# Linear attention of a two-layer decoder: the gate's input by products of 32 columns, four side by side, and heads that begin when the head in front has issued its products

## The chip, the cores and the metric

The kernel runs on one core of a Trainium2 chip. The metric is the device time of one execution in microseconds (us); lower is better. The median of three runs before the change is 1902.51 us.

## The reference, cut to what matters

The program is a trunk of two decoder layers over 528 tokens (16 meta tokens and 512 others) of 1024 features, in float32. Layer 0 is: half a feed-forward network, chunked gated linear attention, half a feed-forward network. Layer 1 has sliding-window attention in the place of the linear attention. The change lies in the linear attention:

```python
def gla_mixer(hn, w_in, w_gate, b_gate, g_head, w_out):
    q, k, v, r, lr = jnp.split(hn @ w_in, [...], axis=-1)   # 512, 512, 1024, 1024, 16 columns
    gk = jax.nn.log_sigmoid((lr @ w_gate + b_gate).astype(jnp.float32)) / GLA_TAU
    ...
    bcum = jnp.cumsum(chunks(padf(gk), GLA_DK), axis=3)
    q_dec = qf * jnp.exp(bcum)
    k_dec = kf * jnp.exp(-bcum)
    att = jnp.where(causal, jnp.einsum('bhncd,bhnsd->bhncs', q_dec, k_dec), 0.0)
    o_intra = jnp.einsum('bhncs,bhnsv->bhncv', att, vf)
    ...                                                       # state passed from chunk to chunk
    o = o_intra + jnp.einsum('bhncd,bhndv->bhncv', q_dec, states)
    o = rmsnorm(o, g_head) * jax.nn.silu(r.astype(jnp.float32)).reshape(B, L, GLA_HEADS, GLA_DV)
    return o.reshape(B, L, GLA_V).astype(hn.dtype) @ w_out
```

`hn` is the normalised residual stream. There are 4 heads with 128 key and 256 value features each. `lr` has 16 columns; its product with `w_gate` gives the forget gate of every key feature.

## The kernel before

Activations are kept transposed: 128 features on the partitions, tokens along the row. The residual stream is `H` (8 tiles of 128 features by 528 tokens), and `Y` is a second array of that size, which holds values, head outputs and projections. Tokens are treated in two groups, `L0 = [(0, 272), (272, 256)]`.

**Products in split precision.** Weights come from memory in units of 128 output columns by 1024 input features (512 KB, two transfers of 256 KB). ScalarE copies each half into a rounded part and VectorE subtracts for the remainder (lines 234 and 235). The operand `x_l0m` is built from `H` in the same way (`Operand.build`, lines 448 and 449): the residual times the norm's gain, without the row factor. `mm3s` makes three products for each 128x128 block (high by high, low by high, high by low), so a unit over both groups is 8 x 3 x 2 = 48 products, `x<-x_l0m,w` in the profile, at line 170 as all products are. The row factor `x.rt` (`R_l0m`) is applied when a result is read out of PSUM; it is ready per group only after sums of squares, a small root on POOL and a broadcast product (`st_l0m`, `r_l0m`).

**Order.** TensorE's order is fixed when the program is built. `Flow` is a planner with a clock: every product advances it by an estimated cost, and generators (jobs) that `yield` a delay or another job are resumed when the clock has come to it (`flow.pump()`, called between products). The constants at the head of the file (`BEHIND`, `ADDED`, `CHAIN` and so on) are such delays. The other engines' orders come from the tile framework, by dependences and program order. SBUF scratch is a pool of 32 equal buffers (`pair_tile`; `duo` gives the two halves of one), PSUM has 8 banks (`ps`). Weight units are loaded ahead in the order of the list `units`, as far as `set_ahead` allows.

**The linear attention, `gla`.** `GLA_ORDER` gives the order of the 25 units of the input weight: unit 24 holds the 16 columns for `lr`, filled up with zeros to 128; 4 to 7 are k, 0 to 3 q, 8 to 15 v, 16 to 23 r.
- `x_first` makes the products of four units together, first for group 0 and then for group 1, as `x_l0m` is built: `lr`, k and q of head 0, and the first v tile. Their results are evacuated when the row factor of the group is done (the jobs `drained`).
- `gates` waits for those, multiplies `lr` with `w_gate` (products `z`, 128 rows of which 16 hold something), and forms the log-sigmoid with Abs, Tanh and Ln on ScalarE and a few operations on VectorE.
- The second v tile is one unit of `x_units`, which makes its products at once and hands the evacuation to a job where the row factor is late.
- `core(h)` is one head: two running sums of the gate (`TENSOR_TENSOR_SCAN`), transposed values (`pv`, `pm`), decayed keys and queries (`d`, `f`, `c`; Exp on ScalarE, products on VectorE), transposed keys (`pk`), scores (`pa`, `pb`), chunk states (`ps`), outputs (`po`, `pn`), and then the head's norm: squares on ScalarE, sums (`st_go`), root, broadcast (`r_go`) and scaling of `Y`. In the last head the two squared tiles of a group are summed by TensorE and the root is on VectorE; in the others POOL adds them and has the root.
- The loop spawns `core(h)`, which waits for the gates, for late evacuations and for the whole of `core(h-1)`, and then makes the four units of the next head, between whose products the planner puts those of `core(h)`.
- Eight units of r follow (`gated`): silu, times the head's normalised output, split into `og`. A tile waits for its own head if that is head 0 or 1, and for the last head otherwise. Then comes the output projection (`y<-og`).

Of the kernel before, what the change touches and what calls it, by code (L numbers as in the profile page):

```python
# [13 lines left out]
ALU = mybir.AluOpType  # L14
AX = mybir.AxisListType

P = 128
D = 1024
KD = 8
# [7 lines left out]
HEADS = 4  # L27
RSQRT_MAGIC = float(0x5F3759DF)
L0 = [(0, 272), (272, 256)]
# [16 lines left out]
ADDED = 1.4  # L46
LONGER = 0.8
BEHIND = 2.2
NORM = 4.0
SHUT = 5.0  # L50
LAG = 5
PERIOD = 3.2
SLOWER = 4.0
# [5 lines left out]
V_GAIN = 0  # L59
# [2 lines left out]
V_GN = 108  # L62
V_SINK = 110
V_N = 126
GLA_ORDER = [24, 4, 0, 8, 9, 5, 1, 10, 11, 6, 2, 12, 13, 7, 3, 14, 15] + list(range(16, 24))


class Flow:
# [63 lines left out]
def trunk_kernel(ctx: ExitStack, tc, a, out):  # L132
    nc = tc.nc
    pe, act, dve, pool, sp = nc.tensor, nc.scalar, nc.vector, nc.gpsimd, nc.sync
    flow = Flow()
# [7 lines left out]
    H = cp.tile([P, KD, TOK], F32, name="H")  # L143
    Y = cp.tile([P, KD, TOK], F32, name="Y")
    vec = cp.tile([P, V_N], F32, name="vec")
# [12 lines left out]
    def duo(name):  # L158
        t = pair_tile(name, F32)
        return t[:, 0], t[:, 1]  # L160
# [237 lines left out]
    def rstd(sq, n, dim, half, name, eng=pool, more=0.0):  # L398
        yy = root(sq, n, dim, name, eng)
        c, nch = yy.shape  # L400
        dg = sm.tile([P, 272], F32, tag="dg", name=f"dg_{name}", bufs=2)
        eng.tensor_tensor(
            dg[:c, :n].rearrange("p (j c) -> p j c", c=c),
            (hident if half else ident)[:c, :c].unsqueeze(1).to_broadcast([c, nch, c]),
            yy.unsqueeze(2).to_broadcast([c, nch, c]),
            op=ALU.mult,
        )
        yield (DCHAIN if eng is dve else CHAIN) + more
        r = ps(f"r_{name}")
        mm(r[:, :n], ones[:c, :], dg[:c, :n])  # L410
        return r
# [3 lines left out]
    def square_into(sums, src, i, count, name, parts=2):  # L415
        n = src.shape[-1]
        if i == 0 or i == count - 1 and parts == 2:
            sums.append(sm.tile([P, 272], F32, tag="acc", name=f"acc_{name}", bufs=6))
            act.activation(sums[-1][:, :n], src, AF.Square)
            return  # L420
        t = sm.tile([P, 272], F32, tag="sq", name=f"sq_{name}", bufs=2)
        act.activation(t[:, :n], src, AF.Square)  # L422
        pool.tensor_tensor(sums[0][:, :n], sums[0][:, :n], t[:, :n], op=ALU.add)  # L423
# [431 lines left out]
    def gla(x, finish):  # L855
        set_ahead(10)
        with tc.tile_pool(name="gp", bufs=1) as gp:
            wg, att = duo("wg")
            wg = wg[:, :512]
# [8 lines left out]
            def resets():  # L868
# [2 lines left out]
                    pool.memset(mt[:, META::st], 0.0)  # L871
                pool.memset(att, 0.0)
                yield 0
            lr = duo("lr")[0]
            qk, ls = {}, {}

            def evac(kind, h, g, p):
                o, n = g
                r = x.rt[:, o : o + n]
                if kind == "lr":  # L880
                    dve.tensor_tensor(lr[:, o : o + n], p[:, :n], r, op=ALU.mult)
                elif kind in "qk":
                    if h not in qk:
                        qk[h] = duo(f"qk{h}")
                    d = qk[h][kind == "k"][:, o : o + n]
                    if kind == "q":
                        dve.scalar_tensor_tensor(d, p[:, :n], 128 ** -0.5, r, op0=ALU.mult, op1=ALU.mult)
                    else:
                        dve.tensor_tensor(d, p[:, :n], r, op=ALU.mult)
                else:  # L890
                    dve.tensor_tensor(Y[:, h, o : o + n], p[:, :n], r, op=ALU.mult)

            def gates(drained):
                for j in drained:
# [22 lines left out]
            blk = lambda t: t[:, META:].rearrange("p (b c) -> p b c", c=P)  # L917

            def core(h, before):
                last = h == HEADS - 1  # L920
                for j in before:
                    yield j
                tau = 1.0 / 16.0
# [96 lines left out]
                for gi, (o, n) in enumerate(L0):  # L1020
                    accs.append([])
                    for i in range(2):
                        square_into(accs[gi], Y[:, 2 * h + i, o : o + n], i, 2, f"go{h}_{gi}", 1 + last)
                yield 2.0 + (0 if last else ADDED)
                def scale(gi, o, n):
                    eng, more = (dve, gi * BEHIND) if last else (pool, BEHIND)
                    r = yield from rstd(accs[gi], n, 256, True, f"go{h}_{gi}", eng, more)
                    dve.tensor_tensor(
                        yy[:, :, o : o + n], yy[:, :, o : o + n],
                        r[:, :n].unsqueeze(1).to_broadcast([P, 2, n]), op=ALU.mult,  # L1030
                    )
# [3 lines left out]

            og, rg = [None] * KD, [None] * KD
            cores = []

            def gated(m, g, p):
                o, n = g  # L1040
# [10 lines left out]
                dve.scalar_tensor_tensor(gs, gs, gn, Y[:, m, o : o + n], op0=ALU.mult, op1=ALU.mult)  # L1051
                split(og[m], gs, g)

            kinds = [("lr", 0), ("k", 0), ("q", 0), ("v", 0)]
            drained = x_first(x, 4, lambda i, g, p: evac(*kinds[i], g, p), first_ahead=5)
            flow.spawn(resets())
            gate = flow.spawn(gates(drained))
            late = x_units(x, 1, L0, lambda i, g, p: evac("v", 1, g, p))
            for h in range(HEADS):
                cores.append(flow.spawn(core(h, [gate] + late + cores[h - 1 : h])))  # L1060
                if h + 1 < HEADS:
                    kk = [("k", h + 1), ("q", h + 1), ("v", 2 * h + 2), ("v", 2 * h + 3)]
                    late = x_units(x, 4, L0, lambda i, g, p, kk=kk: evac(*kk[i], g, p))
# [357 lines left out]
def _tiles(w, kt, mt):  # L1421
    return w.reshape(kt, P, mt, P).transpose(2, 1, 0, 3).reshape(mt, P, kt * P)


def _layout(x, meta_tokens, norm_gains, w_ffn_in, w_ffn_out, gla_w_in, gla_w_gate, gla_b_gate, gla_norm,
            gla_w_out, kv_norm, w_kv, swa_w_q, swa_sinks, swa_w_out):
    c = {}
    c["h"] = np.concatenate([meta_tokens, x[0]], axis=0).T.reshape(KD, P, TOK).transpose(1, 0, 2)
    c["w_in"] = (
        w_ffn_in.reshape(2, 2, KD, P, 2, NFF, P).transpose(0, 1, 5, 4, 3, 2, 6).reshape(2, 2, NFF, 2, P, D)  # L1430
    )
    wo = w_ffn_out.reshape(2, 2, NFF, P, KD, P).transpose(0, 1, 4, 3, 2, 5)
    c["w_out"] = wo[:, :, :, :, :LAST].reshape(2, 2, KD, P, LAST * P)
    c["w_last"] = (
        wo[:, :, :, :, LAST:].transpose(0, 1, 2, 4, 3, 5).reshape(2, 2, NLAST, KD, P, P)
        .transpose(0, 1, 2, 4, 3, 5).reshape(2, 2, NLAST, P, D)
    )
    gin = np.zeros((D, 25 * P), np.float32)
    gin[:, : gla_w_in.shape[2]] = gla_w_in[0]
    c["gla_in"] = _tiles(gin, KD, 25)  # L1440
    wg = np.zeros((P, 512), np.float32)
    wg[:16] = gla_w_gate[0]
    c["w_gate"] = wg
    c["gla_out"] = _tiles(gla_w_out[0], KD, KD)
    c["w_kv"] = _tiles(w_kv, KD, 4)
    c["w_q"] = (
        swa_w_q[0].reshape(KD, P, 2, 2, 4, 64).transpose(2, 4, 1, 0, 3, 5).reshape(KD, P, D)
    )
    c["swa_out"] = (
        swa_w_out[0].reshape(2, 2, 4, 64, 4, 2, P).transpose(0, 4, 1, 3, 5, 2, 6).reshape(KD, P, D)  # L1450
    )
    vec = np.zeros((P, V_N), np.float32)
    vec[:, V_GAIN : V_GAIN + 96] = norm_gains.reshape(96, P).T
    vec[:, V_KVN : V_KVN + 8] = kv_norm.reshape(8, P).T
    vec[:, V_BG : V_BG + 4] = gla_b_gate[0].reshape(4, P).T
    vec[:, V_GN : V_GN + 2] = gla_norm[0].reshape(2, P).T
    vec[:, V_SINK : V_SINK + 16] = np.broadcast_to(
        swa_sinks[0].reshape(2, 2, 4).transpose(0, 2, 1).reshape(1, 16), (P, 16)
    )
    c["vec"] = vec  # L1460
    i, j = np.arange(P)[:, None], np.arange(P)[None, :]
    c["ident"] = np.eye(P, dtype=np.float32)
    c["gmask"] = ((i <= j) & (i // 64 == j // 64)).astype(np.int32)
    c["mgt"] = (j > i).astype(np.int32)
    c["mle"] = (i <= j).astype(np.float32)
    c["rowmask"] = (i // META == np.arange(8)[None, :]).astype(np.float32)
    ang = np.arange(TOK, dtype=np.float32)[:, None] * np.array(INV_FREQ, np.float32)[None, :]
    cos, sin = np.cos(ang).T.astype(np.float32), np.sin(ang).T.astype(np.float32)
    ct, st = np.ones((P, TOK), np.float32), np.zeros((P, TOK), np.float32)
    for r in (0, 64):  # L1470
        ct[r : r + 8], ct[r + 8 : r + 16] = cos, cos
        st[r : r + 8], st[r + 8 : r + 16] = -sin, sin
    c["cos"], c["sin"] = ct, st
    c["sel"] = np.zeros((P, 32), np.float32)
    for e in range(2):
        c["sel"][64 * e : 64 * e + 16, 16 * e : 16 * e + 16] = np.eye(16)
    c["cosp"], c["sinp"] = np.tile(np.concatenate([cos, cos]), (8, 1)), np.tile(np.concatenate([-sin, sin]), (8, 1))
    return {n: np.ascontiguousarray(v) for n, v in c.items()}
# [20 lines left out]
```

## Time and profile before

| | us |
|---|---|
| median of 3 runs (1901.91 to 1903.7) | 1902.51 |
| profiled execution | 1902.08 |
| its span | 1900.2 |
| first and last input product of the linear attention | 376.5 and 577.3 |

The profile is one execution, recorded by the hardware. In a row of the timeline the columns are: start and length in us from the span's start, engine, line, operation, result and operands, shapes and count; what stands in brackets at the end is the idle time in front and who ended it. Neighbouring rows of TensorE overlap, since products are pipelined; a slot is measured from start to start. A full fp32 product is recorded as two instructions, one in split precision (fp32r) as one.

### The profile page before, as it was taken

The page shows a single profiled execution, that of the slowest core. Times are in us where ns is not written, and L with a number is a line of the kernel's source. Part 1 is how long each engine was busy: PE and PEld are TensorE (multiplying, and loading weights), DVE is VectorE, ACT ScalarE, POOL GpSimd, SP SyncE. Part 2 cuts the span into 40 slices and gives each one's busy share as a digit, 9 for nine tenths or more (in the row PEclk, how much of TensorE's full clock was granted, in tenths as well). Part 3 has the DMA queues.
Part 4 walks back from the last instruction along what each step waited for, and adds up shares of the span by engine and source line. Part 5 has one row for each costly group of instructions (what it writes and reads, how often), then busy time and mean ns, then how long its engine had stood idle before and what let it go on. Part 6 is the DMA issues. An engine that isn't in the chain of part 4 may idle for free.

```text
span 1900.2 us, 37641 instructions
## 1 busy us (share of the span) xinstructions
PE 1876.1 (99%) x14642; PEld 1795.0 (94%) x14642; DVE 1403.1 (74%) x2825; ACT 1016.7 (54%) x2268; POOL 189.7 (10%) x374
## 2 busy tenths in 40 slices
PE   8999999999999999999999999999999999999997
PEld 8999999999999999999999898989987898989897
DVE  6885858766574798585887886868766779868584
ACT  5653536653245565363574553535756855636363
POOL 2000000321111300000033000000320140000002
PEclk9999999999999999999999999999999999999999
DMA  4333333422113123333351223233421212333331
GB/s 164 96 98 102 92 105 99 130 79 73 51 57 111 46 79 95 100 95 105 97 178 45 67 85 116 90 111 100 134 73 51 68 46 73 107 103 106 101 112 45
DMA packets 102931, 175.13 MB, mean 92 GB/s; under 512 B 11872, under 2 KB 24928, under 8 KB 102752
## 3 DMA queue, kind: packets, MB, share of 16 engines
q1 hardware_dynamic: 101920, 172.07, 28.9%
q8 instruction: 115, 1.88, 0.4%
q10 hardware_dynamic: 832, 0.65, 0.1%
q14 instruction: 64, 0.52, 0.1%
HBM read 170.05 MB, written 2.10 MB: 91 GB/s over the span
## 4 chain that ended last, share of the span: by engine, by line
PE 87%; DVE 8%; ACT 2%; issue 2%; POOL 0%; DMA 0%; SPq 0%; DVEq 0%; ACTq 0%; POOLq 0%
PE y L170 29%; PE a L170 19%; PE x L170 18%; PE c L170 8%; PE d L170 5%; DVE raw L259 1%; PE o L170 1%; ACT w_s L253 1%; DVE w_s L254 1%; DVE w L254 1%; PE e L170 1%; DVE w L235 1%; PE po L170 1%; PE sa L170 1%; PE ps L170 0%
## 5 line engine op out<-in xcount | busy, mean ns | idle before, releaser
L254 DVE TENSOR_TENSOR w_s<-raw,w_s 128x512 fp32r<-128x512 f32 x288 | 193.7, 690 | 130.5 <-ACT w_s L253 127.9
L170 PE MATMUL y<-hidl0f,w 128*128 128x256 f32 (+1 forms) x2112 | 262.3, 285 | 1.1 <-DVE hidl0f L428 0.9
L170 PEld LDWEIGHTS y<-hidl0f,w 128*128 128x128 f32 x2112 | 259.2, 188 | 2.2 <-DVE hidl0f L428 1.5
L253 ACT ACTIVATE w_s<-raw 128x512 fp32r<-128x512 f32 x288 | 175.1, 628 | 150.8 <-DVE raw L259 137.7
L235 DVE TENSOR_TENSOR w<-raw,w 128x512 fp32r<-128x512 f32 x378 | 236.3, 655 | 21.8 <-ACT w L234 20.0
L170 PE MATMUL y<-hidl1f,w 128*128 128x512 f32 (+1 forms) x1344 | 250.8, 346 | 0.3
L170 PEld LDWEIGHTS y<-hidl1f,w 128*128 128x128 f32 x1344 | 212.3, 188 | 34.9 <-DVE hidl1f L848 1.5
L234 ACT ACTIVATE w<-raw 128x512 fp32r<-128x512 f32 x378 | 207.5, 586 | 41.3 <-PE y L170 29.3
L423 POOL TENSOR_TENSOR acc_post<-acc_post,sq_post 128x256 f32<-128x256 f32 (+1 forms) x77 | 63.6, 826 | 1471.9 <-ACT sq_post L422 1471.2
L259 DVE TENSOR_TENSOR raw<-raw,raw 128x512 f32<-128x512 f32 x288 | 197.9, 687 | 5.5
L254 DVE TENSOR_TENSOR w<-raw,w 128x512 fp32r<-128x512 f32 x216 | 148.2, 687 | 29.9 <-ACT w L253 29.1
L170 PE MATMUL x<-x_l0m,w 128*128 128x272 f32 (+1 forms) x1200 | 158.2, 288 | 0.0
L253 ACT ACTIVATE w<-raw 128x512 fp32r<-128x512 f32 x216 | 134.0, 621 | 41.4 <-PE y L170 41.1
L170 PEld LDWEIGHTS x<-x_l0m,w 128*128 128x128 f32 x1200 | 149.3, 189 | 1.0
L625 DVE TENSOR_TENSOR Y<-y,Y 128x256 f32<-128x256 f32 (+2 forms) x176 | 82.3, 473 | 72.3 <-PE y L170 71.7
L170 PE MATMUL a<-zl0f_t,w_s 128*128 128x264 f32 x864 | 117.3, 285 | 0.0
L170 PE MATMUL a<-zl1f_t,w_s 128*128 128x256 f32 x864 | 114.7, 282 | 0.9 <-ACT c L823 0.8
L170 PEld LDWEIGHTS a<-zl0f_t,w_s 128*128 128x128 f32 x864 | 110.2, 188 | 0.2 <-ACT c L823 0.2
L170 PEld LDWEIGHTS a<-zl1f_t,w_s 128*128 128x128 f32 x864 | 107.4, 188 | 2.7 <-ACT c L823 2.3
L170 PE MATMUL x<-x_l0f,w 128*128 128x256 f32 (+1 forms) x768 | 100.7, 292 | 6.8 <-ACT w L234 6.0
L170 PEld LDWEIGHTS x<-x_l0f,w 128*128 128x128 f32 x768 | 97.6, 193 | 8.0 <-ACT w L234 6.0
L170 PE MATMUL x<-x_l1f,w 128*128 128x256 f32 (+1 forms) x576 | 93.0, 321 | 0.0
(497 smaller groups left out, 3243.9 us busy)
## 6 DMA issues: line engine op xcount, KB each, us to landing
raw<-in_w_in SPq DMA_DIRECT2D x352, 256.0 KB, 2.9
raw<-in_w_out SPq DMA_DIRECT2D x96, 256.0 KB, 3.4
raw<-in_gla_in SPq DMA_DIRECT2D x50, 256.0 KB, 3.2
raw<-in_w_last SPq DMA_DIRECT2D x48, 256.0 KB, 3.1
raw<-in_w_out SPq DMA_DIRECT2D x64, 128.0 KB, 2.9
raw<-in_gla_out SPq DMA_DIRECT2D x16, 256.0 KB, 2.7
raw<-in_w_q SPq DMA_DIRECT2D x16, 256.0 KB, 3.7
raw<-in_swa_out SPq DMA_DIRECT2D x16, 256.0 KB, 3.4
```

Of the source, the lines that this page charges most:

```text
L170: inst = pe.matmul(o, lhs, rhs, start=start, stop=stop, skip_group_check=onto)
L234: act.activation(w[:, 0, :m], raw[:, :m], AF.Copy)
L235: dve.tensor_tensor(w[:, 1, :m], raw[:, :m], w[:, 0, :m].bitcast(F32), op=ALU.subtract)
L253: act.activation(w[:, 0, :512], src, AF.Copy)
L254: dve.tensor_tensor(w[:, 1, :512], src, w[:, 0, :512].bitcast(F32), op=ALU.subtract)
L259: dve.tensor_tensor(dst, dst, src, op=ALU.add)
L423: pool.tensor_tensor(sums[0][:, :n], sums[0][:, :n], t[:, :n], op=ALU.add)
L625: dve.tensor_tensor(y, p[:, :n], y, op=ALU.add)
```

## The change

It has two parts.

The gate's input no longer has a unit of its own. The 16 columns of `lr` are padded to 32 and come unsplit in one block, `w_low` (128 x 8 x 32, 128 KB), which VectorE multiplies by the norm's gain. `low_rank` then multiplies it with `H` in full fp32, 8 products of 32 columns per token group: contraction tile k writes the PSUM partitions of strip k % 4, so that four products lie side by side, and each strip sums two tiles. `w_gate` stands four times on the partitions, so that the gate product `z` sums the four strips. The results are read out when both row factors are done, and `gates` waits for that too. The place of the old unit in `x_first` is taken by the second v tile, and no unit is made behind it before the units of head 1.

A head now waits for `mids[h-1]`, a job that the head in front finishes right behind its last output products and squares, in place of the whole of that head. The last head is treated as the others: POOL adds its squares and has the root.

```diff
-GLA_ORDER = [24, 4, 0, 8, 9, 5, 1, 10, 11, 6, 2, 12, 13, 7, 3, 14, 15] + list(range(16, 24))
+GLA_ORDER = [4, 0, 8, 9, 5, 1, 10, 11, 6, 2, 12, 13, 7, 3, 14, 15] + list(range(16, 24))
...
-            lr = duo("lr")[0]
+            lr, low = duo("lr")
+            low = low[:, : KD * 32].rearrange("p (k c) -> p k c", c=32)
+            sp.dma_start(low, a["w_low"])
...
-                if kind == "lr":
-                    dve.tensor_tensor(lr[:, o : o + n], p[:, :n], r, op=ALU.mult)
-                elif kind in "qk":
+                if kind in "qk":
...
+            def low_rank():
+                gains = vec[:, V_GAIN + 16 : V_GAIN + 16 + KD]
+                dve.tensor_tensor(low, low, gains.unsqueeze(2).to_broadcast([P, KD, 32]), op=ALU.mult)
+                yield LOW
+                banks = [ps(f"lr_{o}") for o, _ in L0]
+                for (o, n), p in zip(L0, banks):
+                    for k in range(KD):
+                        c = slice(k % 4 * 32, k % 4 * 32 + 32)
+                        mm(p[c, :n], low[:, k], H[:, k, o : o + n], k < 4, k >= 4, cost=0.14)
+                for job in x.rjob:
+                    yield job
+                for (o, n), p in zip(L0, banks):
+                    dve.tensor_tensor(lr[:, o : o + n], p[:, :n], x.rt[:, o : o + n], op=ALU.mult)
...
             def core(h, before):
-                last = h == HEADS - 1
...
-                        square_into(accs[gi], Y[:, 2 * h + i, o : o + n], i, 2, f"go{h}_{gi}", 1 + last)
-                yield 2.0 + (0 if last else ADDED)
+                        square_into(accs[gi], Y[:, 2 * h + i, o : o + n], i, 2, f"go{h}_{gi}", 1)
+                mids[h].finish(flow)
+                yield 2.0 + ADDED
                 def scale(gi, o, n):
-                    eng, more = (dve, gi * BEHIND) if last else (pool, BEHIND)
-                    r = yield from rstd(accs[gi], n, 256, True, f"go{h}_{gi}", eng, more)
+                    r = yield from rstd(accs[gi], n, 256, True, f"go{h}_{gi}", pool, BEHIND)
...
+            mids = [Job(None) for _ in range(HEADS)]
...
-            kinds = [("lr", 0), ("k", 0), ("q", 0), ("v", 0)]
+            kinds = [("k", 0), ("q", 0), ("v", 0), ("v", 1)]
             drained = x_first(x, 4, lambda i, g, p: evac(*kinds[i], g, p), first_ahead=5)
             flow.spawn(resets())
-            gate = flow.spawn(gates(drained))
-            late = x_units(x, 1, L0, lambda i, g, p: evac("v", 1, g, p))
+            gate = flow.spawn(gates(drained + [flow.spawn(low_rank())]))
+            late = []
             for h in range(HEADS):
-                cores.append(flow.spawn(core(h, [gate] + late + cores[h - 1 : h])))
+                cores.append(flow.spawn(core(h, [gate] + late + mids[h - 1 : h])))
...
+    low = np.zeros((D, 32), np.float32)
+    low[:, :16] = gla_w_in[0][:, 24 * P :]
+    c["w_low"] = low.reshape(KD, P, 32).transpose(1, 0, 2)
+    wg = np.zeros((4, 32, 512), np.float32)
+    wg[:, :16] = gla_w_gate[0]
+    c["w_gate"] = wg.reshape(P, 512)
```

The new constant `LOW = 1.0` is the planner's delay between the scaling of the block and its products.

More of the change, by code (lines that the diff above doesn't have):

```diff
@@ L50 @@
 SHUT = 5.0
+LOW = 1.0
 LAG = 5
@@ L1437, in _layout @@
     )
[L1438 to L1443, printed above, removed]
+    c["gla_in"] = _tiles(gla_w_in[0][:, : 24 * P], KD, 24)
+    low = np.zeros((D, 32), np.float32)
[4 more added lines that the diff above has]
+    c["w_gate"] = wg.reshape(P, 512)
     c["gla_out"] = _tiles(gla_w_out[0], KD, KD)
```

## The prediction

> **What bounds the kernel now.** I read the page's totals and chain first, then the linear attention stage in the table by stretches, then the waits of TensorE in that stage, and last its timeline, because the change touches no other stage.
>
> ```profile
> span 1900.2 us, 37641 instructions
> ...
> PE 1876.1 (99%) x14642; PEld 1795.0 (94%) x14642; DVE 1403.1 (74%) x2825; ACT 1016.7 (54%) x2268; POOL 189.7 (10%) x374
> ...
> PE 87%; DVE 8%; ACT 2%; issue 2%; POOL 0%; DMA 0%; SPq 0%; DVEq 0%; ACTq 0%; POOLq 0%
> ```
>
> TensorE is busy for 99% of the span and carries 87% of the chain that ended last. The table by stretches (columns: stretch, length, then busy time of PE, PEld, DVE, ACT, POOL) covers the stage:
>
> ```profile
> 376.50:400.00 23.50, 23.50 (x195) 23.37 (x194) 18.86 (x51) 14.87 (x37) 12.93 (x28) 1.00 0.12 35
> 400.00:427.00 27.00, 27.00 (x211) 26.43 (x210) 15.07 (x31) 13.08 (x22) 3.28 (x13) 1.00 0.34 108
> 427.00:466.00 39.00, 39.00 (x316) 37.71 (x315) 23.08 (x44) 13.43 (x28) 8.18 (x27) 1.00 0.22 69
> 466.00:506.00 40.00, 40.00 (x324) 38.51 (x323) 20.64 (x41) 12.60 (x27) 6.60 (x27) 1.00 0.21 66
> 506.00:546.00 40.00, 40.00 (x324) 38.58 (x323) 26.94 (x61) 15.93 (x38) 8.36 (x27) 1.00 0.13 41
> 546.00:578.00 32.00, 32.00 (x263) 30.68 (x262) 23.29 (x69) 13.88 (x31) 0.00 (x0) 1.00 0.22 67
> ```
>
> From 376.5 to 578 us TensorE has no idle time and the granted clock is 1.00; VectorE is at 52 to 80%, ScalarE at 32 to 63%. The waits of TensorE in and around the stage are one, at its end:
>
> ```profile
> PE y L170 <- DVE og L428: 0.4, 1, 0.4
> ```
>
> So a product that goes from this stage shortens the kernel by its own slot, as long as no new wait opens. Earlier heads by themselves are worth nothing here: the waits of one head are already filled with input products.
>
> **The products that go.** Unit 24 of the input weight holds 16 useful columns in 128. It takes 8 (contraction) x 3 (split precision) x 2 (token groups of 272 and 256) = 48 products. A run of input products that alternates between both groups gives their slot:
>
> ```profile
> 427.54 8.99 PE L170 MATMUL x<-x_l0m,w 128*128 128x272 f32 x72
> 436.37 0.60 PE L182 MATMUL pk<-ident,f 128*128 128x128 f32 x4
> ```
>
> 72 products take 436.37 - 427.54 = 8.83 us from start to start, 0.1226 each; 48 of them are **5.9 us**. The unit's place among the first four is taken by the second v unit, which was a unit of its own behind them, so nothing else is added or lost there.
>
> **The products that come.** 16 products in full fp32, 128 x 32 weights, 272 or 256 columns, in rounds of four that write partitions 0-31, 32-63, 64-95 and 96-127. The sliding-window part of this kernel has the same form, four products of 32 columns side by side (each recorded as two):
>
> ```profile
> 1392.69 0.64 PE L170 MATMUL turn<-q,sel 128*32 128x256 f32 x8
> 1393.26 2.97 PE L170 MATMUL x<-x_l1m,w 128*128 128x256 f32 x23
> ...
> 1441.57 1.06 PE L170 MATMUL turn<-q,sel 128*32 128x512 f32 x8
> 1442.56 0.30 PE L182 MATMUL ptm<-ident,mt 128*64 128x128 f32 x1
> ...
> L170 PEld LDWEIGHTS turn<-q,sel x24: 106/108/109, 1392.7 to 1441.6; 128*32 128x32 f32 x24
> ```
>
> Four at 256 columns hold TensorE for 0.57 us, four at 512 for 0.99. That is 0.42 us per 256 columns and 0.15 us fixed. Two rounds at 272 (0.60) and two at 256 (0.57) make **2.3 us**. The lower bound pays the fixed part once: 2 x 0.45 + 2 x 0.42 + 0.15 = 1.9. The upper bound puts the 0.108 us weight load of the last row in front of every one of the 8 passes on top of 2.3, 3.2. I take 2.3, since the rows have the same shape and precision.
>
> The Trainium skill ("TensorE: Matmul & The Clock Gate", Part 3, The mechanism) says that a weight load overlaps running products only when its row group differs, and here all four strips use all rows; by that rule all eight loads would show, and the block would be an estimated 1.74 us of columns and 8 x 0.108, 2.6 us. The trace speaks against it mildly: the two loads of a round, with the change of shape, cost 0.15 us together, less than 2 x 0.108.
>
> **The rest of the low-rank path.** The 32 columns come by one 128 KB transfer issued at the head of the stage, right behind the gate weight. Nothing is queued behind it on SyncE that is urgent, as its timeline shows:
>
> ```profile
> 361.68 0.33 SPq L860 DMA_DIRECT2D wg<-in_w_gate  x1
> 395.14 10.14 SPq L302 DMA_DIRECT2D raw<-in_gla_in  x12
> ...
> wg<-in_w_gate SPq DMA_DIRECT2D x1, 256.0 KB, 2.6
> ```
>
> The next weight is issued long after it, and the gate weight landed in 2.6 us, so the block is there well before it is used at about 402 us. It occupies half of a buffer that was taken anyhow for the low-rank result, though some 30 us earlier. VectorE scales it once (256 elements per partition, about 0.4 us), and loses two of the 128x512 splits of the old unit; ScalarE loses two copies. Cost on the path: zero, bounded by 0.5 us above if VectorE reaches the scaling late behind weight splits, and zero below, as TensorE waits for neither today.
>
> The evacuation of the low-rank result moves behind both row factors. The first group used to be done early; now both follow the second factor:
>
> ```profile
> 415.31 1.94 PE L170 MATMUL z<-lr,wg 128*128 128x272 f32 x8
> ...
> 411.89 0.42 DVE L881 TENSOR_TENSOR lr<-x,R_l0m 128x256 f32<-128x256 f32 x1 [2.95 <-ACT R_l0m L471]
> ```
>
> The gate products z start 3.0 us after that evacuation ended (412.31), because the planner waits for all drains of the first four units, which stay. One or two operations of 0.42 us more in front fit into the 3.0 us. Cost zero; the gates, and so head 0, begin when they do now.
>
> **The heads.** Head h+1 is released where head h has issued its last products, not where its normalisation is done. For heads 0 and 1 that is, in the timeline:
>
> ```profile
> 424.34 0.60 PE L182 MATMUL pv<-ident,Y 128*128 128x128 f32 x4
> ...
> 451.48 5.00 PE L170 MATMUL x<-x_l0m,w 128*128 128x256 f32 x39
> ...
> 466.24 0.60 PE L182 MATMUL pv<-ident,Y 128*128 128x128 f32 x4
> ...
> 475.75 0.60 PE L182 MATMUL pk<-ident,f 128*128 128x128 f32 x4
> ```
>
> A head takes 27 us from its first transposes (424.3) to its last products (451.5), and 14.8 us more until the next begins (466.2). Head 1 can begin at 451.5; its own input units are then issued, since they stand one unit further forward. Head 2 follows at 479 and head 3 at 506, or up to 6 us later where its input units come later than that. Its products then end by 539 and its normalisation by 554, some 20 us before the input products, which end near 578 now, the end of the last stretch of the table, and about 4 us earlier then. TensorE does the same products in another order, so the sum is zero, with two exceptions at the end.
>
> First, the last head now forms its sum of squares as the others do, by adding on POOL, which halves the products of that step:
>
> ```profile
> 456.32 1.04 PE L170 MATMUL st_go<-ones,acc_go 128*68 128x1 f32 x12
> ...
> 572.96 1.98 PE L170 MATMUL st_go<-ones,acc_go 128*68 128x1 f32 x24
> ```
>
> 1.98 us becomes 1.04: **0.94 us** less. The root on POOL in place of VectorE is longer, but the 20 us behind it cover that.
>
> Second, the one wait of the stage goes:
>
> ```profile
> 580.75 35.29 PE L170 MATMUL y<-og,w 128*128 128x272 f32 x283 [0.38 <-DVE og L428]
> ...
> 578.30:590.00 11.70, 11.28 (x89) 10.81 (x88) 11.23 (x25) 9.04 (x23) 0.00 (x0) 1.00 0.31 90
> ```
>
> VectorE is at 96% there, because the gated tiles 4 to 7 all wait for the last head. They are then spread over the input units before: **0.38 us** less, at best. Late next is the last gated tile alone, hidden behind the first output products.
>
> **Sum:** -5.9 + 2.3 - 0.94 - 0.38 = -4.9 us. The profiled execution took 1902.08 us for its span of 1900.2; the median of the runs is 0.43 above it. 1902.51 - 4.9 = **1897.6 us**.
>
> **The rivals.** *The four strips run one after another.* Then a round costs four times its 0.57, and the block 9.3 us: +9.3 - 5.9 - 0.94 - 0.38 = +2.1, 1904.6 us, no measurable change. The turn rows speak against it (four products in the time of one and a bit); what they don't have is an accumulation of two rounds into one strip. Chance 0.05.
>
> *The handover opens small waits.* A head's vector work has only a limited cover. For head 0, which began its scans with nothing in front of it, the rows on VectorE are:
>
> ```profile
> 427.88 1.25 DVE L926 TENSOR_TENSOR_SCAN b<-resets,ls 128x528 f32<-128x528 f32 x1
> ...
> 434.19 0.57 DVE L954 TENSOR_TENSOR f<-f,qk 128x400 f32<-128x400 f32 x1
> ...
> 453.18 1.25 DVE L926 TENSOR_TENSOR_SCAN b<-resets,ls 128x528 f32<-128x528 f32 x1
> ```
>
> That is 6.9 us from scan to the keys f that the transposes pk need. For head 1 pk stands 9.5 us behind pv, and its scans ran 13 us ahead of pv. With the new order the scans may lose that lead, and then 2.6 us of cover are left, shared with the normalisation of the head in front on ScalarE and the weight splits on VectorE. One us lost at each of three handovers gives 1900.6 us, by the bound below no change. VectorE's 52 to 59% in the stretches from 427 to 506 speaks against it. Chance 0.22.
>
> *The handover becomes the bound (slower).* The same mechanism, beyond its cover: ScalarE first does the tail of the head in front, VectorE first the weight splits, and the keys come late. From a delay of 2.6 us on TensorE stops, and from 2.6 + 2.9 = 5.5 us per handover the three cost 8.7 us, net +3.8. With 6 us of delay the three cost 10.2: 1907.8 us; at 7 us it would be 1910.8. For it: the operations share buffers that the head in front frees only with its last products. Against it: over 40% of VectorE and two thirds of ScalarE are idle in those stretches. Chance 0.13.
>
> **How the numbers follow.** A measurement of this kernel can tell 0.2%, 3.8 us, from no change: faster is below 1898.7, slower above 1906.3. The forecast has the remaining 0.60; its own range is 1896.0 to 1898.7. The lower end takes 0.4 us for the block at 1.9, 0.6 us if the 283 output products (35.29 / 283 = 0.1247 each) come down to the 0.1226 of the input products once VectorE is less crowded beside them, and 0.6 us of scatter, the distance of the fastest run, 1901.91, from the median. The 8-in-10 range goes up into the small waits, to 1901.8, and leaves out the slower rival, the serial strips and a little on either side. Faster 0.62 (the forecast and the mildest small waits), same 0.25, slower 0.13.
>
> **What would show it.** In the changed profile: 1152 input products in place of 1200; 32 records of the new products in about 2.3 us, starting within 30 ns of one another by fours; z within 1 us of where it stands; pv of head 1 near 451 us; the last head's r_go 15 us or more before the first y<-og; no wait there; and y<-og starting 4 to 5 us earlier. The prediction is wrong if TensorE shows waits ahead of pk, pa or pv, or if the new products wait for their scaled block.

## The result, and the profile after

The changed kernel takes **1896.94 us** (median of 7 runs, 1895.95 to 1897.11) against 1903.14 us for the kernel before (7 runs), 6.2 us less; the ratio is 0.9965, 95% interval 0.9956 to 0.9975. The prediction was 1897.6 us in a range of 1896.0 to 1901.8, with 0.62 on faster by over 0.2%. Ratios, here and below, are of fast runs; one run of e5_heads_later, 3353.32 us at a mean clock of 0.786, was in a slower state and stands in no ratio.

The page's totals and chain, after:

```profile
span 1895.3 us, 37597 instructions
...
PE 1871.5 (99%) x14614; PEld 1789.4 (94%) x14614; DVE 1400.4 (74%) x2802; ACT 1015.6 (54%) x2268; POOL 199.1 (11%) x400
...
PE 87%; DVE 8%; ACT 2%; issue 1%; POOL 0%; DMA 0%; DVEq 0%; ACTq 0%; POOLq 0%
```

TensorE is still the bound, with 28 records less (48 input products and 12 sum records go, 32 come). The stage in the table by stretches:

```profile
400.00:427.00 27.00, 27.00 (x227) 25.40 (x226) 14.53 (x30) 13.85 (x24) 2.76 (x12) 1.00 0.26 87
427.00:466.00 39.00, 39.00 (x320) 37.41 (x319) 26.67 (x56) 16.33 (x35) 9.00 (x27) 1.00 0.20 68
466.00:506.00 40.00, 40.00 (x314) 37.72 (x312) 24.49 (x47) 14.24 (x32) 10.87 (x30) 1.00 0.21 67
```

The list of TensorE's waits from 360 to 690 us, whole:

```profile
PE y L171 <- DVE hidl0f L429: 0.3, 1, 0.3
```

TensorE has no idle time; the wait at the first output products is gone, and the one that is left belongs to the feed-forward part behind. VectorE and POOL are busier from 427 to 506 us, where heads now overlap. The timeline of TensorE:

```profile
376.00 4.29 PE L171 MATMUL x<-x_l0m,w 128*128 128x272 f32 x33
...
403.62 1.99 PE L171 MATMUL lr<-H,lr 128*32 128x272 f32 x32
405.54 4.30 PE L171 MATMUL x<-x_l0m,w 128*128 128x272 f32 x33
...
450.76 0.60 PE L183 MATMUL pv<-ident,Y 128*128 128x128 f32 x4
...
551.95 1.06 PE L171 MATMUL r_go<-dg_go,ones 68*128 68x272 f32 x4
552.65 20.41 PE L171 MATMUL x<-x_l0m,w 128*128 128x256 f32 x165
572.90 36.71 PE L171 MATMUL y<-og,w 128*128 128x272 f32 x297
609.44 0.60 PE L171 MATMUL st_post_l0f<-ones,acc_post 128*68 128x1 f32 x8
```

The stage, from the first input product to the first output product, lasts 572.90 - 376.00 = 196.90 us, where it was 201.64 (376.63 to 578.27): -4.74. The first part of the output projection, up to st_post_l0f, lasts 36.54, where it was 37.60 (578.27 to 615.87): -1.06. So the change is worth 5.8 us in the trace. The span falls by 4.9. Two differences outside this stretch make up the rest: the opening was 0.63 us shorter, which adds to the gain, and later the granted clock was halved for one stretch, which the execution before did not have and which takes more away. TensorE's timeline where it starts:

```profile
1513.39 0.44 PE L171 MATMUL o<-pt,dv 128*64 128x128 f32 x4 [0.88 <-DVE pt L1288]
```

The stretch behind it in the table (the last columns are the granted clock, 0.50, and the DMA's share and rate):

```profile
1514.90:1518.20 3.30, 3.30 (x16) 2.79 (x14) 1.54 (x5) 0.50 (x2) 0.00 (x0) 0.50 0.00 0
```

It lies in the sliding-window part, behind a wait that both kernels have, and set the rest of the program back by 1.55 us, as the shift between the two traces shows (counted from the first product, 6.16 us ahead in front of it, 4.61 behind it).

### The profile page after: what moved, and what is told of

Same layout as the page of the kernel before. It is cut to its first block, busy times and chain, and to the rows that moved or that the text cites. A ratio compares the mean times of both kernels' runs of the same rounds, so it can differ in the third digit from the quotient of the medians.

```text
span 1895.3 us, 37597 instructions
## 1 busy us (share of the span) xinstructions
PE 1871.5 (99%) x14614; PEld 1789.4 (94%) x14614; DVE 1400.4 (74%) x2802; ACT 1015.6 (54%) x2268; POOL 199.1 (11%) x400
## 4 chain that ended last, share of the span: by engine, by line
PE 87%; DVE 8%; ACT 2%; issue 1%; POOL 0%; DMA 0%; DVEq 0%; ACTq 0%; POOLq 0%
PE y L171 29%; PE a L171 19%; PE x L171 18%; PE c L171 8%; PE d L171 5%; DVE raw L260 1%; PE o L171 1%; ACT w_s L254 1%; DVE w_s L255 1%; DVE w L255 1%; PE e L171 1%; DVE w L236 1%; PE po L171 1%; PE sa L171 1%; PE ps L171 0%
## 5 line engine op out<-in xcount | busy, mean ns | idle before, releaser
L171 PE MATMUL x<-x_l0m,w 128*128 128x272 f32 (+1 forms) x1152 | 152.3, 289 | 0.0
L171 PEld LDWEIGHTS x<-x_l0m,w 128*128 128x128 f32 x1152 | 143.5, 189 | 1.5 <-issue 0.4
```

Of the source, the lines that this page charges most:

```text
L171: inst = pe.matmul(o, lhs, rhs, start=start, stop=stop, skip_group_check=onto)
```

## The experiments

The stage's length and the listed waits at r_go, the broadcast of a head's norm, are the two numbers to compare, each from one profile; the ratios are against the kernel before on the same chip, whose median was 1903.02 us for e1 to e4, 1902.92 for e5 to e9 and 1903.90 for e10 and e11.

| kernel | median us | ratio, 95% interval | stage us | wait at r_go us |
|---|---|---|---|---|
| before | 1903.14 | | 201.64 | none |
| changed | 1896.94 | 0.9965 (0.9956 to 0.9975) | 196.90 | none |
| e1_low_alone | 1909.25 | 1.0033 (1.0020 to 1.0045) | 207.71 | 6.8 |
| e2_heads_alone | 1904.80 | 1.0012 (1.0004 to 1.0021) | 206.12 | 3.4 |
| e3_last_on_pe | 1903.32 | 1.0001 (0.9992 to 1.0010) | 202.60 | 2.9 |
| e4_one_strip | 1906.09 | 1.0018 (1.0009 to 1.0027) | 205.97 | 2.2 |
| e5_heads_later | 1902.09 | 0.9992 (0.9983 to 1.0002) | 200.59 | none |
| e6_earlier | 1899.90 | 0.9984 (0.9976 to 0.9993) | 200.95 | 2.3 |
| e8_margin | 1899.77 | 0.9984 (0.9975 to 0.9993) | 199.97 | 1.4 |
| e9_last_dve_later | 1897.69 | 0.9970 (0.9959 to 0.9981) | 197.84 | none |
| e10_later | 1898.44 | 0.9968 (0.9956 to 0.9981) | 196.83 | none |
| e11_roots_dve | 1896.18 | 0.9963 (0.9949 to 0.9976) | 196.85 | none |

**e1_low_alone: the low-rank part alone.** Against the changed kernel (the lines of the last head's sums and root are those of before as well):

```diff
-                cores.append(flow.spawn(core(h, [gate] + late + mids[h - 1 : h])))
+                cores.append(flow.spawn(core(h, [gate] + late + cores[h - 1 : h])))
```

> The changed kernel with its second part undone: a head waits for the whole of the head in front, and the last head has its squares summed by TensorE and its root on VectorE, as before. Theory (two separate sums of TensorE slots): 48 input products of 5.9 us go, the block of 1.92 us comes, so 4.0 us faster than the kernel before; the last head ends with the input products as before, and the first 18 output products again lose about 1.1 us to late gated tiles. Rival (the low-rank part gains only because the heads were moved with it): under 2 us faster, with a new wait of TensorE in front of the gates or of the first head.

It is 6.2 us slower than the kernel before. The theory falls: the products are saved, and more is lost. Of the rival the main part holds, no gain without the moved heads, but the new waits are not in front of the gates or of the first head. From the list of TensorE's waits:

```profile
PE r_go L171 <- DVE dg_go L403: 5.4, 1, 5.4
...
PE r_go L171 <- POOL dg_go L403: 1.4, 1, 1.4
```

The longer one is at the last head. TensorE's timeline at the end of the stage:

```profile
574.85 1.98 PE L171 MATMUL st_go<-ones,acc_go 128*68 128x1 f32 x24
582.20 2.13 PE L171 MATMUL r_go<-dg_go,ones 68*128 68x272 f32 x4 [5.36 <-DVE dg_go L403]
```

The table by stretches there:

```profile
579.50:586.00 6.50, 3.80 (x13) 3.39 (x14) 5.44 (x23) 0.43 (x1) 0.00 (x0) 0.50 0.22 76
```

The input products are out when the last head asks for its norm: between st_go and r_go nothing is issued, TensorE waits 5.4 us for VectorE's root, and the clock is halved from within that wait on. In the kernel before, input products still stood between the two, and the four heads, one behind the other, ended together with them:

```profile
574.81 2.79 PE L170 MATMUL x<-x_l0m,w 128*128 128x256 f32 x21
577.46 1.16 PE L170 MATMUL r_go<-dg_go,ones 68*128 68x272 f32 x4
578.27 2.10 PE L170 MATMUL y<-og,w 128*128 128x272 f32 x14
```

Taking 4 us of products away lays the heads' own chain bare. The chain also grew: the wait of 1.4 us, at head 2, comes from POOL's small operations, which last 8.0 us together there (6.0 in the kernel before), and a stretch of half clock follows it.

**e2_heads_alone: the heads alone.** The kernel before with `mids`, and the last head treated as the others:

```diff
-                cores.append(flow.spawn(core(h, [gate] + late + cores[h - 1 : h])))
+                cores.append(flow.spawn(core(h, [gate] + late + mids[h - 1 : h])))
```

> The kernel before with the second part alone: heads released behind the products of the head in front, the last head with POOL's adding and root; the low-rank columns still have their unit of 48 products. Theory: 0.94 us for the last head's sums and 1.1 us for the output products that no longer meet late gated tiles, 2.0 us faster than before, and about 4 us slower than the changed kernel. Rival (earlier heads are worth something by themselves, or nothing without the freed slots): 4 us or more faster, or within 0.5 us of before.

1.8 us slower than before: neither theory nor rival. POOL's, VectorE's and TensorE's timelines around the longer of its two waits, with one row of the kernel before ahead of them:

```profile
459.54 0.23 POOL L388 TENSOR_SCALAR wv_go<-wv_go 68x4 f32<-68x4 f32 x1
```

That is the operation in head 0 of the kernel before; in e2, head 1:

```profile
486.41 4.42 POOL L388 TENSOR_SCALAR wv_go<-wv_go 68x4 f32<-68x4 f32 x1
490.81 0.19 POOL L381 TENSOR_TENSOR wv_go<-wv_go,zv_go 128x2 f32<-128x2 f32 x1
...
485.56 0.72 DVE L944 TENSOR_TENSOR d<-d,qk 128x528 f32<-128x528 f32 x1 [2.93 <-ACT d L943]
...
490.34 0.41 DVE L959 TENSOR_TENSOR c<-c,qk 128x256 f32<-128x256 f32 x1
490.67 0.75 DVE L889 TENSOR_TENSOR qk<-x,R_l0m 128x272 f32<-128x272 f32 x2
...
494.10 1.05 PE L170 MATMUL r_go<-dg_go,ones 68*128 68x272 f32 x2 [2.60 <-POOL dg_go L402]
```

The stretch behind it in the table:

```profile
494.40:497.70 3.30, 3.30 (x13) 2.73 (x12) 2.29 (x4) 1.66 (x4) 0.48 (x1) 0.50 0.07 9
```

A POOL operation on 68 x 4 numbers, 0.2 us elsewhere, lasts 4.42 us. While it does, VectorE works almost without a pause from SBUF operands (486.54 to 490.67), on the next head's keys and queries and on two weight splits; here POOL goes on when VectorE comes to an evacuation, whose first operand lies in PSUM. In the kernel before the same chain of head 0 ran while VectorE had nothing but two such evacuations, and its 22 small operations took 4.3 us together; here those of head 1 take 9.6. So r_go, whose place among TensorE's products is fixed, is reached before POOL is done, and the clock is halved right behind. The Trainium skill ("GPSIMD Engine Reference", 1. Specifications) says that GpSimd's SBUF interfaces are shared with VectorE, in contention with instructions that have two SBUF inputs; the rows agree with it.

**e5_heads_later** puts r_go behind that delay (e2 with one more line changed):

```diff
-                    r = yield from rstd(accs[gi], n, 256, True, f"go{h}_{gi}", pool, BEHIND)
+                    r = yield from rstd(accs[gi], n, 256, True, f"go{h}_{gi}", pool, BEHIND + 3.0)
```

> The heads alone, as in e2, but the planner puts the broadcast r_go of each head 3 us later among the input products. Theory (what e2 lost is the wait at r_go, because POOL's root is held up by VectorE's work for the next head, and half a window of clock behind it): no wait at r_go, no halved clock there, and the two gains of 0.94 and 1.1 us come out: 2.0 us faster than the kernel before. Rival (earlier heads cost TensorE something by themselves): still slower than the kernel before by 1 us or more, without a wait at r_go.

POOL is held up as before (10.2 us in head 1), but in TensorE's timeline the wait is gone:

```profile
481.84 1.05 PE L170 MATMUL st_go<-ones,acc_go 128*68 128x1 f32 x12
...
495.10 1.16 PE L170 MATMUL r_go<-dg_go,ones 68*128 68x272 f32 x4
...
576.79 36.72 PE L170 MATMUL y<-og,w 128*128 128x272 f32 x297
613.35 0.60 PE L170 MATMUL st_post_l0f<-ones,acc_post 128*68 128x1 f32 x8
```

A stretch of the same execution in the sliding-window part:

```profile
1517.40:1524.00 6.60, 6.60 (x37) 5.27 (x34) 3.21 (x11) 1.20 (x3) 0.00 (x0) 0.50 0.00 0
```

The stage is 1.05 us shorter than before and the projection 1.04 (36.56 for 37.60): the 2.0 us of the theory. The median moves by 0.8 us only and its interval reaches no change; the profiled execution has at least these 6.6 us at half clock in the sliding-window part, which the heads do not touch. The gain in the stage is shown, that of the whole time is not settled.

**e3_last_on_pe and e9_last_dve_later: the last head.** The changed kernel with the last head's sums on TensorE and its root on VectorE, and the same with that root's r_go later:

```diff
... (the last head's sums on TensorE, as before)
-                    r = yield from rstd(accs[gi], n, 256, True, f"go{h}_{gi}", pool, BEHIND)
+                    eng, more = (dve, gi * BEHIND) if last else (pool, BEHIND)          # e3
+                    eng, more = (dve, 5.0 + gi * BEHIND) if last else (pool, BEHIND)    # e9
+                    r = yield from rstd(accs[gi], n, 256, True, f"go{h}_{gi}", eng, more)
```

> The changed kernel, but the last head's squares are summed by TensorE and its root is on VectorE, as before. Theory: the sums' 0.94 us come back and nothing else, since the last head ends 20 us ahead of the input products either way: 0.9 us slower than the changed kernel, 5.1 us faster than before, still no wait at the first output products. Rival (POOL's root is what spread VectorE's work at the end): the 1.1 us of late gated tiles come back too, 4 us faster than before.

> As e3 (the last head's squares summed by TensorE, its root on VectorE), with that head's r_go put 5 us later. Theory: the wait of 2.9 us at its r_go and the halved clock behind it go, and what is left of the difference to the changed kernel are the 12 more records of st_go, 0.94 us: 5.1 us faster than the kernel before. Rival (VectorE's root delays the gated tiles or the weights): 4 us faster or less.

The timeline of TensorE in e3 at the last head:

```profile
549.75 1.24 PE L171 MATMUL r_go<-dg_go,ones 68*128 68x272 f32 x2 [2.93 <-DVE yv_go L387]
```

The stretch behind it in the table:

```profile
549.80:553.10 3.30, 3.30 (x13) 3.07 (x14) 1.13 (x2) 0.00 (x0) 0.00 (x0) 0.50 0.35 98
```

e3 missed, theory and rival: not 0.9 but 6.4 us slower than the changed kernel. VectorE's root is held up in its own queue (its small operations take 5.7 us from first to last, 1.9 in the kernel before), r_go waits 2.93 us, and half clock follows. e9 takes the wait away: 5.2 us faster than before, and its stage is 0.94 us longer than that of the changed kernel, the 0.94 of the sums. From e3 to e9 the stage falls by 4.76 us for a wait of 2.93; a stretch of 3.4 us at half clock, an estimated 1.7 us lost, is nearly all of the rest.

**e4_one_strip: the strips one after another.**

```diff
-                        c = slice(k % 4 * 32, k % 4 * 32 + 32)
-                        mm(p[c, :n], low[:, k], H[:, k, o : o + n], k < 4, k >= 4, cost=0.14)
+                        mm(p[:32, :n], low[:, k], H[:, k, o : o + n], k == 0, k == KD - 1, cost=0.5)
... (the result and the gate product z use 32 rows)
```

> The changed kernel with all 8 products of a token group in one strip of 32 columns, so that no two can lie side by side; the gate product then has 32 rows in place of 128. The planner is told 0.5 us for each product. Theory (the four strips run at the same time): each product now needs about 0.48 us by itself (two passes of 0.24), 16 of them 7.7 us in place of 1.92, so 5.8 us slower than the changed kernel, within 1 us of the kernel before. Rival (products of 32 columns are cheap by their width alone): the block stays under 3 us and the time within 1 us of the changed kernel.

TensorE's timeline (a slot runs from start to start):

```profile
404.18 7.31 PE L171 MATMUL lr<-H,lr 128*32 128x272 f32 x32
411.42 0.70 PE L171 MATMUL r_l0m<-dg_l0m,ones 128*128 128x256 f32 x2
```

The block takes 7.24 us in place of 1.92 (403.62 to 405.54): the theory's 7.7 nearly, and the rival falls. Side by side is worth 5.3 us. The time is 9.2 us above the changed kernel, though, and not 5.8. Of the 9.1 us by which the stage is longer, TensorE's slots give the block 5.3, the waits at r_go of heads 0 and 1, which came with the shift in its order, 2.2, the gate products z, now of 32 rows, 0.8, and the input products 0.6.

**e6_earlier: the next head released before the output products.**

```diff
+                mids[h].finish(flow)
                 pm = ps(f"pn{h}")
...
-                mids[h].finish(flow)
                 yield 2.0 + ADDED
```

> The changed kernel, but the next head is released before the output products po of the head in front are issued, some 5 us earlier. Theory A (what decides is POOL's root beside VectorE's key preparation): the preparation is over before the root begins, POOL's small operations of heads 0 and 1 are back at 0.2 us each, r_go has 1 us or more to spare, and the time is that of the changed kernel within 0.7 us. Rival B (the handover is bounded by the buffers that the head in front frees with its last products): TensorE waits in front of pv, pk or pa by 1 us or more per head, 3 us or more slower than the changed kernel.

The timelines of POOL, VectorE and TensorE in head 1:

```profile
481.14 3.37 POOL L382 TENSOR_TENSOR wv_go<-wv_go,zv_go 68x4 f32<-68x4 f32 x1
484.59 0.48 POOL L381 TENSOR_SCALAR wv_go<-zv_go 128x2 f32<-128x2 f32 x1
...
484.45 0.58 DVE L971 TENSOR_TENSOR f<-f,qk 128x400 f32<-128x400 f32 x1
484.94 0.76 DVE L890 TENSOR_TENSOR qk<-x,R_l0m 128x272 f32<-128x272 f32 x2
...
489.18 1.28 PE L171 MATMUL r_go<-dg_go,ones 68*128 68x272 f32 x2 [2.34 <-POOL dg_go L403]
```

3 us slower than the changed kernel, and both fail in part: there is no wait in front of pv, pk or pa, so the buffers are not the bound; but the preparation is not over when POOL begins, and the wait is at r_go once more. POOL's long operation ends at 484.51 here, 0.4 us ahead of VectorE's next evacuation, so an operand in PSUM is not what lets POOL go on in every case.

**e8_margin and e10_later: r_go moved by 1 us.** `BEHIND - 1.0` and `BEHIND + 1.0` in the line shown for e5.

> The changed kernel with r_go put 1 us earlier by the planner. In the changed kernel POOL's dg_go ends 0.1 to 0.4 us ahead of r_go in heads 0 and 1. Theory (that margin is all there is): waits of 0.6 to 0.9 us at r_go in heads 0 and 1, 1.5 us slower than the changed kernel, 3 us or more where the clock is halved behind a wait. Rival (POOL's chain would follow, or the waits are taken back elsewhere): within 0.5 us of the changed kernel.

> The changed kernel with r_go put 1 us later by the planner. Theory (the changed kernel has no wait at r_go, only a margin of 0.1 to 0.4 us): nothing to gain, within 0.7 us of the changed kernel, 1896.9, and no wait at r_go. Rival (short waits below what the profile's list of waits shows are left in the changed kernel): 1 us or more faster than it.

In the changed kernel head 1's dg_go ends at 489.23 and r_go starts at 489.33 us, in the timelines of POOL and TensorE:

```profile
488.59 0.64 POOL L403 TENSOR_TENSOR dg_go<-hident,yv_go 68x272 f32<-68x272 f32 x1
...
489.33 0.67 PE L171 MATMUL r_go<-dg_go,ones 68*128 68x272 f32 x2
```

In e8, 1 us earlier, TensorE waits in both heads:

```profile
462.70 1.54 PE L171 MATMUL r_go<-dg_go,ones 68*128 68x272 f32 x4 [0.56 <-POOL dg_go L403]
490.41 1.54 PE L171 MATMUL r_go<-dg_go,ones 68*128 68x272 f32 x4 [0.89 <-POOL dg_go L403]
```

The waits are as expected, 0.56 and 0.89 us, but the price is not: the stage is 3.1 us longer and the time 2.8, at full clock, where 1.5 was expected. From start to start the two r_go come 0.73 and 1.04 us later behind their neighbours than in the changed kernel. The r_go of the second token group is late too, in heads 0, 1 and 3, by idle times of 0.10 to 0.12 us that the list does not show; the slots of all r_go grow by another 1.1 us together. e10 has the stage of the changed kernel to 0.07 us and no wait; its median is 1.5 us above, outside what was expected. Its five runs are 1895.4 and 1895.9 us at a mean clock of 0.998, and 1898.4, 1899.2 and 1899.8 at 0.995 to 0.996, so that excess goes with the clock; where the slower three lost it was not recorded, since the stage is that of the first run alone.

**e11_roots_dve: the roots on VectorE, with r_go as early as in e8.**

```diff
-                    r = yield from rstd(accs[gi], n, 256, True, f"go{h}_{gi}", pool, BEHIND)
+                    r = yield from rstd(accs[gi], n, 256, True, f"go{h}_{gi}", dve, 3.2)
```

> As e8 (r_go 1 us earlier than in the changed kernel), but every head's root runs on VectorE in place of POOL. Theory (r_go is late in e8 because POOL's small operations are stretched beside VectorE's dense work): VectorE needs 3.6 us for the root where POOL needed 7 to 9, the waits of 0.56 and 0.89 us at r_go go, and the time is that of the changed kernel within 0.7 us, 1897. Rival (VectorE's own queue is the bound, as at the last head of e3): waits at r_go of 1 us or more, 1900 or slower.

The timelines of VectorE and TensorE in head 1:

```profile
487.31 0.42 DVE L403 TENSOR_TENSOR dg_go<-hident,yv_go 128x256 f32<-128x256 f32 x1
...
488.23 1.06 PE L171 MATMUL r_go<-dg_go,ones 68*128 68x272 f32 x4
```

The waits of e8 go, by nothing but the engine of the root. From its first operation to the last dg_go VectorE needs 6.4 us in head 1, not the 3.6 expected, but POOL needed 8.5 in the changed kernel. The time, 1896.18 us, is the lowest of all, but its ratio can't be told from that of the changed kernel; its use is that r_go stands 1 us earlier and still has 0.5 us to spare.

## Why the prediction was right, step by step

- **The bound.** That TensorE's slots set the time held for the changed kernel. The condition put to it, "as long as no new wait opens", breaks as soon as the low-rank part stands alone: in e1 the heads in series are as long as the input products, which the rows at 578 us could have told. The 4 us are had only because the heads are released earlier (e1 undoes the last head's treatment as well, but that alone, in e9, is worth 0.94 us of the stage). Equally, "earlier heads by themselves are worth nothing" missed that they give the room for it.
- **48 products, 5.9 us.** Adding up the start-to-start slots of all input products gives 151.4 us before and 145.6 after: 5.75.
- **The block, 2.3 us.** It is 1.92, the lower bound. The fixed part of a round was the mis-sized term: within the block the fours start 7 ns apart and the next four 0.20 to 0.23 us later, with no price for the change of weights; 0.11 of the 0.15 of the turn rows is paid once, at the change of shape behind the block (a last slot of 0.309 us, where the others between fours are 0.20). The prediction also misread the loads: it counted two a round and 8 in all, but the turn rows have 8 a round (24 in three runs of products), and the block has 32, of 0.106 to 0.110 us. If all of them had shown, its upper bound would have been 5.8 us in place of 3.2; the block's 1.92 leaves no room for them. The estimate of 2.6 by the Trainium skill's rule on weight loads ("TensorE: Matmul & The Clock Gate", Part 3, The mechanism) would have been 5.2; the trace does not agree with the rule here.
- **The rest of the low-rank path, nothing.** Right: the block's scaling was done at 379.8 us, 24 us ahead of its use, and z began 1.2 us earlier, where the stage began 0.6 earlier.
- **The sums of the last head, 0.94.** e9 shows exactly that.
- **The last wait, 0.38.** It was 1.06. The list named one wait, but in the kernel before five of the first 18 output products had start-to-start slots of 0.23 to 0.66 us, where 0.125 is usual, all from 578.3 to 581.7 us, while VectorE was still making gated tiles. In the changed kernel these 18 have 0.12 to 0.13 each. The 0.6 that the lower end had set aside was for the other output products, and those did not get faster.
- **The places.** Head 1 at 450.8 (forecast 451.5), heads 2 and 3 at 477.3 and 513.7 (479, and 506 to 512, so the last is 1.7 us later than the latest that was forecast), the last r_go 21 us ahead of the first output product (20).
- **The rivals.** Serial strips: refused by the trace, priced by e4 at 5.3 us for the block. Small waits at the handover: that a head's vector work can delay TensorE was right, the place was wrong. The prediction looked at VectorE's chain to pk, and no kernel here waits in front of pk; what is short is POOL's root of the head in front, which is held up beside VectorE's dense work for the next head. It spared the changed kernel by 0.1 us, in a place where the prediction had not looked: that no wait opened there was luck. The slower rival's price per handover left out the halved clock, and e2 shows that two such waits, with one stretch at half clock, are enough to turn 2 us of gain into 1.8 us of loss.

The sum was 4.9 us; the trace has -5.75 + 1.92 - 0.94 - 1.06 = -5.8. The forecast of the time, 1897.6 us, came nearer to the measured 1896.94 than the sum did to the change, 4.9 for 6.2 in the medians, because the three runs that it started from had a median 0.63 us below that of all seven.

## What to carry to other kernels

Where an order is fixed ahead, a part that saves slots on the bound engine has to be judged together with the serial chain that ends beside it: here either half of the change alone, as it stands, is slower, and both together are faster (the heads alone are slower only through the place of r_go: with it 3 us later, e5, their stage is 1.05 us shorter than before). Look for chains that end in the same microsecond as the work you shorten, and for the margin between each producer and the fixed place of its consumer; 0.1 us is as good as 1 until something else is moved. In this kernel small POOL chains did well where VectorE had pauses (4.3 us) and badly beside its dense work (7 to 10 us); moved to VectorE they were in time in e11, but late in e3, behind VectorE's other work.

## What the runs showed of the hardware

- **Four products of 32 columns side by side cost little more than one.** 16 full fp32 products with different weights take 1.92 us by fours and 7.24 one behind the other (e4), a factor of 3.8.
- **A wait of TensorE costs more than itself.** During or right behind waits of 1.43 to 5.36 us at r_go in e1, e2, e3 and e6, and behind one of 0.88 among narrow products in the sliding-window part, the granted clock is halved for stretches that the trace's record of the clock gives as 3.41 or 6.83 us. Behind waits of 0.56 to 1.37 us at r_go in e2, e4 and e8, and of 1.20 to 1.45 at r_kv, some 1030 us into every kernel, it stays full, so the length of the wait alone does not decide. The stretches of full clock in front of the next change are whole multiples of 3.4133 us (30.72, 365.23, 1396.05). The Trainium skill ("TensorE: Matmul & The Clock Gate", Part 1) has a free-running window of 3.4 us and the half clock behind an idle window of that length; the stretches agree with the window, but here the drop came with less idle time than that too, with 0.88 us in the changed kernel, e3, e5 and e9; what else counts was not tried. The same wait of 0.88 us stands in the other eight traces at full clock. Within nearly every kernel the longer runs are those with the lower mean clock, as in e10, so that much of the scatter of 3 to 4 us goes with it.
- **POOL can stop while VectorE streams SBUF operands:** 0.2 us became 4.42 in e2 and 3.37 in e6. What lets it go on is open: in e2 it did when VectorE came to an operand in PSUM, in e6 0.4 us ahead of one, and the operand's place was not tried by itself.
